# The chunk scan of an S5 layer: steps over chunk pairs against one hardware scan per 16 groups in a turned frame

## The chip, the cores and the metric

One core of one Trainium2 chip runs the whole program in one launch. Its engines are PE (matmuls, "PEld" its weight loads), DVE (vector), ACT (scalar functions and copies), POOL (GpSimd, elementwise work at leisure) and SP, which here only issues transfers. POOL issues transfers too, so a transfer in its queue stands behind the arithmetic issued before it. The metric is the device time of one execution in microseconds (us). A run of the kernel before takes 1603.12 us (median of 3; 1601.82 to 1603.6).

## The reference

One inference step of two decoder layers of width 1024 over 512 prompt tokens and 8 sample sequences of 8 tokens. Layer 0 mixes tokens with HGRN2 (a gated recurrence with 8 heads of 128), layer 1 with S5 (a complex diagonal recurrence). Every layer goes on with a SwiGLU mixer and a gated per-layer embedding, with LayerNorms after the residuals. The part that the change is about:

```
lam = lax.complex(a_re, a_im)                       # 64 groups x 64 states
lam_bar = jnp.exp(lam * delta)                      # the decay of one token
b_bar = ((lam_bar - 1.0) / lam)[..., None] * lax.complex(b_re, b_im)
bu = einsum('btgc,gpc->btgp', u, b_bar)             # 16 channels of a group
bu = bu.at[:, 0].add(lam_bar * h0)
h_t = lam_bar * h_(t-1) + bu_t                      # associative scan over the tokens
y = einsum('btgp,gcp->btgc', h, c_mat).real + d_skip * u
y = gelu(y);  val, gate = split(y @ w_glu);  out = val * sigmoid(gate)
```

Outputs are the features of all tokens, the last HGRN2 states, and the last S5 states of the prompt and of each sample sequence.

## The kernel before

**Tiling.** The 576 tokens go in two blocks of 288 columns, features on the partitions, eight k tiles of 128. Block 0 holds the first 224 prompt tokens and the 64 sample tokens, block 1 the other 288 prompt tokens. Each product with a weight matrix is made of three matmuls (L297 to L299), from a rounded part (`whi`, `xh`) and the rest (`wlo`, `xl`) of both sides. Matmuls write to `mm` banks, of which there are four, and the order of instructions on an engine is that in which the program issues them; an engine waits in order.

**Weight stream.** Slots of 128x1024 are loaded into two `wraw` buffers (`w_dma`, L224, on SP; within the S5 stage on POOL), copied to `whi` by ACT (L198) and taken from the raw values into `wlo` by DVE (L201), by POOL in the S5 stage. A slot's load is issued when its buffer is free, in SP's queue behind what was issued before.

**Preparation of S5.** `s5_prep_steps` is a generator that the channel mixer of layer 0, `ffn(0)`, calls one or two steps at a time between its output tiles. It loads the parameters, makes the decay `lam_bar` = `er` * (`r1` + i `r0`) with an exponential and two sines on ACT (L195), its powers up to 8 (`lr`, `li`) and the coefficients on DVE, and a table that PE transposes (L1222), ACT copies to `wts` and POOL's queue stores to `wt_scratch` (L1225). Then it walks over 16 packs of four groups: `load` issues three loads on SP, `bc` (L1240), `wr` (L1242), which reads `wt_scratch` and so waits for its store, and `bT` (L1246); `inputs` (DVE, from `zw<-wr,bT`) makes the input weights, which POOL's queue stores to `zw_scratch` (L1280); `coeffs` and `lag_kernels` make the output weights (`cl_scratch`) and the products within a chunk (`mg_scratch`). In between the mixer goes on: DVE adds PE's output tiles to the residual (`xf<-xf,mm`, L204), which frees the banks.

**S5 stage.** A chunk is 8 tokens. `U` holds the inputs with rows (step, channel) and columns [group, chunk]; `HS[0]`, `HS[1]` (tiles `xl`) hold the states at the starts of the chunks, real parts on rows 0 to 63, imaginary parts on rows 64 to 127, 64 groups by 36 chunks. Block 0 has chunks 0 to 27 (`KA` = 28) and the 8 sample sequences, one chunk each. In order:
- `z_part(0)`: PE makes what each chunk adds to the state, ACT copies it to `HS` and `ZL`.
- The scan of block 0 on DVE: `many` adds to every other state the one before, advanced by `lam8` (the decay of one chunk); `pair_step` goes in thirteen steps two chunks at a time with `lam16`; `many` then fills in the states between. `advance` is a complex product and a sum in five operations. The temporaries lie in `spare`, in the place of XH of block 1 (named `xh`).
- `ple_proj`: projections of layer 1's embeddings on PE, sixteen tiles, each copied by ACT to `pj`; then POOL issues the load of the samples' initial states `h0` (tile `sm`, L1531), and DVE scales them into `HS[0]` (L1532).
- `z_part(1)`; the samples' last states on POOL (`last_samples`).
- `lag_part` (products within the chunks, both blocks, into `U`) and `out_part(0)` (products of states with the output weights, L1371, added to `U` on DVE, GELU on ACT, stored to scratch and loaded back by `y_load`). Between them `step(scan, ...)` issues pieces of block 1's scan, `last_states`, as many as the tables `SL` and `SO0` say.
- The gated projection: units of block 0 on PE; before the fourth of them what is left of the scan is issued (`settle("scan")`), and then `out_part(1)` for the eight octets.

Of the kernel before, what the change touches and what calls it, by code (L numbers as in the profile page):

```python
# [17 lines left out]
T = 576  # L18
# [49 lines left out]
SL = (0, 1, 1, 1, 1, 1, 1, 0)  # L68
SO0 = (1, 1, 1, 1, 2, 1, 1, 1)
SY0 = (1, 1, 1, 1, 1, 1, 1, 1)  # L70
# [12 lines left out]
def weight_order():  # L83
    """The 128 x 128 weight tiles (name, layer, k tile, first column) as they are consumed."""
# [56 lines left out]
def hybrid_decoder_kernel(ctx: ExitStack, tc: tile.TileContext, a: dict):  # L141
# [16 lines left out]
    # ---------------------------------------------------------------- constants  # L158
# [23 lines left out]
    # features of all tokens; tile k of block b is [:, b, k, :], but for HGRN2, which takes k tiles of all tokens  # L182
# [3 lines left out]
    # the float32r part of a block's features and the rest of them  # L186
# [22 lines left out]
    # ---------------------------------------------------------------- weight stream  # L209
    # Slots are split as buffers come free, paced by the matmuls issued: not before their load has had  # L210
    # time to arrive, not two at once, so that the engines that split them go on with other work.
# [15 lines left out]
    def w_conv(force=False):  # L227
        """Splits the next slot into a float32r part and the rest, if a buffer is free."""
# [73 lines left out]
    def unit(out, p, ks, rh, rl, blk, first=True, last=True):  # L302
        """One output tile of one token block: sum over the k tiles ks with weights from position p."""
# [6 lines left out]
    def units(outs, p, ks, rh, rl, blk):  # L310
        """Output tiles whose weights follow each other, all of them with one k tile before the next."""
# [11 lines left out]
    def tick():  # L323
        """Called every few matmuls: issues a little of what was put off until its inputs are there."""
# [47 lines left out]
    # ---------------------------------------------------------------- norms  # L372
    class LayerNorm:
        """LayerNorm over features of the block's tiles in xf: sums are taken about the mean of the
        first half of the features, which lies within one standard deviation of the mean."""
# [12 lines left out]
        def added(self, m):  # L388
            """Called when tile m of the block is final."""
# [18 lines left out]
        def tail(self):  # L408
# [5 lines left out]
            # squares about the mean of the first half, as the tiles come  # L414
# [55 lines left out]
    # ---------------------------------------------------------------- HGRN2  # L470
    def hgrn():
# [24 lines left out]
        # lower bounds: softmax over the layer axis (one layer), cumulative sum less its first row  # L496
# [26 lines left out]
        def proj(h):  # L523
# [25 lines left out]
        def pairs(x, l):  # L549
            """The first and the second half of each chunk of 2 l prompt tokens."""  # L550
# [8 lines left out]
        def decay(h, d, ps):  # L559
            """Logarithm of the decay, keys, and the decay's sums from the starts of chunks of four sizes."""  # L560
# [86 lines left out]
        def scan(h):  # L647
# [3 lines left out]
            # decayed keys, token-major  # L651
# [13 lines left out]
            # states of the prompt blocks  # L665
# [10 lines left out]
            # states of the sample sequences  # L676
# [14 lines left out]
            # scores, transposed: [s, t]  # L691
# [16 lines left out]
            # what the initial states add to the outputs of the sample sequences: of four sequences, the queries of  # L708
            # all with the state of each
# [13 lines left out]
            # outputs  # L723
# [18 lines left out]
            # RMS norm over the head and output gate  # L742
# [26 lines left out]
        # output projection; the last head's scan runs beside the k tiles of the others  # L769
# [72 lines left out]
    # ---------------------------------------------------------------- channel mixer  # L842
# [104 lines left out]
    # ---------------------------------------------------------------- per-layer embedding  # L947
    def embeddings(i, pool):
        """The layer's input embeddings; the second result splits them once they are loaded."""
# [23 lines left out]
    def ple_gate(i, pj, pp, segs, emit, wait, second=None):  # L973
        """Gates of the projected embeddings for the columns (block, from, to) of each segment, in their order;
        the result starts the norm of a segment. The norms of all segments but the last start by themselves,
# [479 lines left out]
    def layer0_to_1():  # L1455
# [51 lines left out]
        for half in range(2):  # L1507
            many(0, 2, KA // 2 - 1, half)
# [306 lines left out]
```

## Time and profile before

| | |
|---|---|
| Runs | 1603.12 us (1601.82 to 1603.6) |
| Span of the profiled execution | 1598.7 us |
| Median less this span | 4.4 us |
| PE busy | 1516.5 us, 95% of the span |
| DVE / ACT / POOL busy | 941.6 / 688.3 / 238.7 us |
| Preparation of S5, from the first sine's input to the store of `wt_scratch` | about 459 to 500 us |
| S5 stage, scans on DVE | block 0 909 to 948, block 1 948 to 1012 us |

The page splits the span into engines' busy times, groups of instructions (line, engine, operation, output <- inputs) and transfers. A view of waits tells for each engine whom it waited for; a timeline row gives start, duration, engine, line, work, and in brackets the idle time before it and who ended it. A row with "x3" covers three instructions in a row. The name of a tile is that of the first tile in its place or the one written: the states appear as `xl`, the scan's temporaries as `xh`.

### The profile page before, as it was taken

Reading aid. Unit: us, or ns where it says so; the run is one execution under the profiler, and the core shown is the slowest. Engines: PE = TensorE matmul, PEld = TensorE weight load, DVE = VectorE, ACT = ScalarE, POOL = GpSimd, SP = SyncE. Lnnn points to the kernel's source line nnn. Section 1 sums busy time; section 2 is a strip of 40 time slices with the busy share of each in tenths; the row PEclk is TensorE's granted clock in tenths of the full one; section 3 lists DMA queues with packets and bytes.
Section 4 is the critical chain, followed back from the end, with each engine's and each line's share of the span. In section 5 each row is a group of like instructions: output and inputs, shape, how many; then the busy total and the mean of one; then the engine's idle time right before and its main releaser. Section 6 shows DMA issues by size and latency. Waiting matters only on the chain.

```text
span 1598.7 us, 30007 instructions
## 1 busy us (share of the span) xinstructions
PE 1516.5 (95%) x12550; PEld 1469.0 (92%) x12550; DVE 941.6 (59%) x1833; ACT 688.3 (43%) x1159; POOL 238.7 (15%) x284
## 2 busy tenths in 40 slices
PE   7899999899999999999999965899999999999998
PEld 7898989778999999999989965799999999999997
DVE  5748475768547666753476799567533333334685
ACT  5646464646532233123278533336522232133375
POOL 1303020202000112360022432202000000000111
PEclk9999999999999999999999996899999999999999
DMA  5213122232225766752215973332222222223021
GB/s 184 102 61 108 69 100 75 83 114 82 77 73 138 211 190 181 199 156 93 93 67 190 162 281 93 88 106 80 67 80 93 80 80 80 93 80 119 28 79 59
DMA packets 96390, 175.59 MB, mean 110 GB/s; under 512 B 41792, under 2 KB 56816, under 8 KB 96256
## 3 DMA queue, kind: packets, MB, share of 16 engines
q1 hardware_dynamic: 87856, 149.56, 30.2%
q0 software_dynamic: 8400, 24.13, 5.3%
q8 instruction: 98, 1.61, 0.4%
q14 instruction: 36, 0.29, 0.1%
HBM read 148.72 MB, written 24.94 MB: 109 GB/s over the span
## 4 chain that ended last, share of the span: by engine, by line
PE 71%; DVE 18%; ACT 5%; issue 2%; DMA 1%; POOL 1%; SPq 0%; DVEq 0%; ACTq 0%; POOLq 0%
PE mm L297 23%; PE mm L298 22%; PE mm L299 22%; DVE b L576 2%; DVE xh L201 2%; DVE wlo L201 1%; DVE am L201 1%; DVE ac L201 1%; DVE xl L201 1%; DVE K L201 1%; DVE xf L201 1%; ACT whi L198 1%; DVE ln_q L201 1%; DVE ln_z L201 1%; PE tr L668 1%
## 5 line engine op out<-in xcount | busy, mean ns | idle before, releaser
L297 PE MATMUL mm<-xh,whi 128*128 128x288 f32 x2048 | 609.0, 297 | 7.9 <-ACT xh L198 4.4
L298 PE MATMUL mm<-xl,whi 128*128 128x288 f32 x2048 | 607.8, 297 | 4.8 <-POOL xl L201 3.4
L299 PE MATMUL mm<-xh,wlo 128*128 128x288 f32 x2048 | 606.0, 296 | 1.3 <-DVE wlo L201 1.3
L297 PEld LDWEIGHTS mm<-xh,whi 128*128 128x128 f32 x2048 | 387.3, 189 | 14.5 <-ACT xh L198 5.6
L298 PEld LDWEIGHTS mm<-xl,whi 128*128 128x128 f32 x2048 | 387.4, 189 | 7.4 <-POOL xl L201 4.5
L299 PEld LDWEIGHTS mm<-xh,wlo 128*128 128x128 f32 x2048 | 387.3, 189 | 1.5 <-DVE wlo L201 1.5
L198 ACT ACTIVATE whi<-wraw 128x1024 fp32r<-128x1024 f32 x208 | 218.7, 1053 | 226.4 <-PE mm L298 124.2
L201 DVE TENSOR_TENSOR wlo<-wraw,whi 128x1024 fp32r<-128x1024 f32 x200 | 246.1, 1247 | 29.9 <-ACT whi L198 27.1
L297 PE MATMUL mm<-hhi,whi 128*128 128x288 f32 x704 | 209.3, 297 | 0.0
L299 PE MATMUL mm<-hhi,wlo 128*128 128x288 f32 x704 | 207.5, 295 | 0.0
L298 PE MATMUL mm<-hlo,whi 128*128 128x288 f32 x704 | 207.3, 294 | 0.0
L201 DVE TENSOR_TENSOR fs<-fs,mm 128x288 f32<-128x288 f32 x88 | 40.0, 454 | 267.6 <-PE mm L299 258.4
L297 PEld LDWEIGHTS mm<-hhi,whi 128*128 128x128 f32 x704 | 132.1, 188 | 1.7 <-issue 1.4
L298 PEld LDWEIGHTS mm<-hlo,whi 128*128 128x128 f32 x704 | 132.1, 188 | 0.3
L299 PEld LDWEIGHTS mm<-hhi,wlo 128*128 128x128 f32 x704 | 132.0, 188 | 0.0
L297 PE MATMUL mm<-xhi,whi 128*128 128x288 f32 x384 | 122.6, 319 | 0.0
L298 PE MATMUL mm<-xlo,whi 128*128 128x288 f32 x384 | 114.6, 298 | 0.0
L299 PE MATMUL mm<-xhi,wlo 128*128 128x288 f32 x384 | 114.3, 298 | 0.0
L201 POOL TENSOR_TENSOR ln_s<-ln_s,xf 128x288 f32<-128x288 f32 x24 | 24.3, 1011 | 574.4 <-DVE xf L201 454.7
L198 ACT ACTIVATE hhi<-fs 128x288 fp32r<-128x288 f32 x88 | 38.9, 442 | 148.3 <-DVE fs L201 148.3
L195 ACT ACTIVATE fs<-mm,eps 128x288 f32<-128x288 f32 x88 | 44.1, 502 | 135.7 <-PE mm L299 135.6
L297 PEld LDWEIGHTS mm<-xhi,whi 128*128 128x128 f32 x384 | 73.2, 191 | 6.9 <-issue 4.4
(292 smaller groups left out, 2166.3 us busy)
## 6 DMA issues: line engine op xcount, KB each, us to landing
wraw<-in_w_dram SPq DMA_DIRECT2D x198, 512.0 KB
wraw<-in_w_dram POOLq DMA_DIRECT2D x10, 512.0 KB, 5.6
S<-in_s_dram SPq DMA_DIRECT2D x8, 512.0 KB
out_hgs_dram<-So SPq DMA_DIRECT2D x8, 512.0 KB
wr<-wt_scratch SPq DMA_DIRECT2D x16, 256.0 KB
bT<-in_s5bt_dram SPq DMA_DIRECT2D x16, 256.0 KB
cl_scratch<-cl POOLq DMA_DIRECT2D x16, 256.0 KB, 3.4
zw_scratch<-zw POOLq DMA_DIRECT2D x16, 256.0 KB, 6.3
```

The lines of the kernel that those rows point to most:

```text
L195: nc.scalar.activation(out, in_, func, bias=ZERO if bias is None else bias, scale=scale)
L198: nc.scalar.activation(out, in_, ACT.Copy)
L201: (eng or nc.vector).tensor_tensor(out, x, y, op=op)
L297: nc.tensor.matmul(out, whi, rhi, start=start, stop=False)
L298: nc.tensor.matmul(out, whi, rlo, start=False, stop=False)
L299: nc.tensor.matmul(out, wlo, rhi, start=False, stop=stop)
L576: nc.vector.tensor_tensor_scan(b[l], segm[l], L, 0.0, op0=OP.mult, op1=OP.add)
L668: nc.tensor.matmul(ps[:, j * 128:j * 128 + 128], kT[:, j, :], Vh[:, j, :], start=True, stop=True)
```

## The change

The decay of a chunk is written as a length times a direction, `lam8` = `rho` * (c + i z). In a frame that turns with the direction, the recurrence over chunks has the real factor `rho`, the same for real and imaginary parts, and DVE's instruction for a first-order recurrence along a row (`tensor_tensor_scan`) can do it.

1. **Table (in the preparation, all on POOL).** `rho` from `er`; the direction's powers 1, 2, 4 .. 32 chunks by squaring, each brought back to length 1 by one correction (`direction`): 81 operations of 128x64. Then `turns(half)` for each 32 groups: powers 0 to 35, by doubling (36 products and sums of 128x32xn, n = 1, 2, 4, 8, 16, 4), the sign of the imaginary part, and two stores to `tb_scratch`. `turns(0)` is called behind the powers `lr`, `li`, `turns(1)` behind the coefficients, ahead of the table for `wt_scratch`. The tiles of the second half are those of the first. `lam16` with its four DVE operations goes.
2. **Load.** The table (C and Z, 1.18 MB each) comes by SP at the beginning of the S5 stage; Z takes the place of `spare`.
3. **Scan.** For each quarter of 16 groups: `turn` back (four DVE operations), one `tensor_tensor_scan` over 128x576, `turn` forward (four). The factors `rho`, 0 at each group's first chunk, lie in one buffer in the place of an earlier embedding; ACT fills it for the next quarter behind each scan (`lengths`). `SL` and `SO0` hand out block 1's scan in half quarters, seven of them, and what is left is issued before the gated projection begins.
4. **Around it.** `z_part(0)` has one copy less for each octet, and the state at block 1's start is copied once from `HS[0]`; the samples' initial states are scaled by ACT, not by DVE; both blocks' outputs come back into the place of `U[0]`.

```diff
-SL = (0, 1, 1, 1, 1, 1, 1, 0)
-SO0 = (1, 1, 1, 1, 2, 1, 1, 1)
-SY0 = (1, 1, 1, 1, 1, 1, 1, 1)
+SL = (0, 0, 1, 0, 1, 0, 1, 0)
+SO0 = (0, 1, 0, 1, 0, 1, 0, 1)
...
-    lam16 = const.tile([128, 2, NG], FP32, name="lam16")
+    rho = const.tile([128, NG], FP32, name="rho")
+    tb_d = nc.dram_tensor("tb_scratch", (128, 2, NG, 36), FP32).ap()
...
+        P = nc.gpsimd
+        pc, pz = (sp.tile([128, 6, NG], FP32, name=x) for x in ("pc", "pz"))
+        ta, tb = s64("ta"), s64("tb")
+
+        def square(c, z, c0, z0):
+            tt(ta, z0, z0, OP.mult, P)
+            tt(tb, c0, z0, OP.mult, P)
+            tt(c, c0, c0, OP.mult, P)
+            tt(c, c, ta, OP.subtract, P)
+            tt(z, tb, tb, OP.add, P)
+
+        def direction(c, z, first):
+            tt(ta, c, c, OP.mult, P)
+            tt(tb, z, z, OP.mult, P)
+            tt(ta, ta, tb, OP.add, P)
+            P.tensor_scalar(tb, ta, -0.5, 1.5, op0=OP.mult, op1=OP.add)
+            tt(c, c, tb, OP.mult, P)
+            tt(z, z, tb, OP.mult, P)
+            if first:
+                P.tensor_scalar(ta, ta, 0.5, 0.5, op0=OP.mult, op1=OP.add)
+                tt(rho, rho, ta, OP.mult, P)
+
+        tt(rho, er, er, OP.mult, P)
+        for _ in range(2):
+            tt(rho, rho, rho, OP.mult, P)
+        square(pc[:, 0], pz[:, 0], r1, r0)
+        for m in range(8):
+            if m > 1:
+                direction(pc[:, m - 2], pz[:, m - 2], m == 2)
+            if m < 2:
+                square(pc[:, 0], pz[:, 0], pc[:, 0], pz[:, 0])
+            elif m < 7:
+                square(pc[:, m - 1], pz[:, m - 1], pc[:, m - 2], pz[:, m - 2])
+
+        def turns(half):
+            gs = slice(32 * half, 32 * half + 32)
+            C, Z = (sp.tile([128, 32, 36], FP32, tag=x, name=x) for x in ("tC", "tZ"))
+            P.memset(C[:, :, 0:1], 1.0)
+            P.memset(Z[:, :, 0:1], 0.0)
+            for m in range(6):
+                n0 = 1 << m
+                n = min(n0, 36 - n0)
+                sh = [128, 32, n]
+                bc, bz = (x[:, m, gs, None].to_broadcast(sh) for x in (pc, pz))
+                A, B = (sp.tile([128, 32, 16], FP32, tag=x, name=x)[:, :, 0:n] for x in ("tA", "tB"))
+                c0, z0, c, z = C[:, :, 0:n], Z[:, :, 0:n], C[:, :, n0:n0 + n], Z[:, :, n0:n0 + n]
+                tt(A, c0, bc, OP.mult, P)
+                tt(B, z0, bz, OP.mult, P)
+                tt(c, A, B, OP.subtract, P)
+                tt(A, z0, bc, OP.mult, P)
+                tt(B, c0, bz, OP.mult, P)
+                tt(z, A, B, OP.add, P)
+            P.tensor_scalar(Z, Z, NSG, None, op0=OP.mult)
+            nc.gpsimd.dma_start(tb_d[:, 0, gs], C)
+            nc.gpsimd.dma_start(tb_d[:, 1, gs], Z)
...
+        turns(0)
...
-        tt(lam16[:, 0], lr[:, 8], lr[:, 8], OP.mult)
...
+        turns(1)
...
+    def turn(blk, q, back):
+        gs, n = slice(16 * q, 16 * q + 16), slice(1, 36 if blk else KA + 1)
+        h, c, C, Z = (x[:, n] if len(x.shape) == 2 else x[:, :, n] for x in
+                      (HS[blk][:, gs], s5["c"], s5["C"][:, gs], s5["Z"][:, gs]))
+        tt(c[0:64], h[64:128], Z[64:128], OP.mult)
+        tt(c[64:128], h[0:64], Z[0:64], OP.mult)
+        tt(h, h, C, OP.mult)
+        tt(h, h, c, OP.add if back else OP.subtract)
+
+    def lengths(q):
+        copy(s5["rho"][:, :, 1:36], rho[:, 16 * q:16 * q + 16, None].to_broadcast([128, 16, 35]))
+
+    def run_on(blk, q):
+        h = HS[blk][:, 16 * q:16 * q + 16].rearrange("p g k -> p (g k)")
+        nc.vector.tensor_tensor_scan(h, s5["rho"].rearrange("p g k -> p (g k)"), h, 0.0, op0=OP.mult, op1=OP.add)
+        lengths((q + 1) % 4)
...
-        for half in range(2):
-            many(0, 2, KA // 2 - 1, half)
-        for j in range(1, KA - 1, 2):
-            pair_step(j)
-        for half in range(2):
-            many(0, 1, KA // 2 - 1, half)
+        for q in range(4):
+            turn(0, q, True)
+            run_on(0, q)
+            turn(0, q, False)
+        copy(HS[1][:, :, 0], HS[0][:, :, KA])
...
-        nc.vector.tensor_scalar(HS[0][:, :, KA:36], h0, NSG, None, op0=OP.mult)
+        act(HS[0][:, :, KA:36], h0, ACT.Identity, scale=NSG)
...
-            for half in range(2):
-                many(1, 0, 18, half)
+            for q in range(4):
+                turn(1, q, True)
+                run_on(1, q)
                 yield
-            for j in range(KA - 1, 63, 2):
-                pair_step(j)
...
+                turn(1, q, False)
                 yield
...
-        tails["scan"] = scan
+        run(scan)
```

How the instructions move. First POOL's queue in the preparation; a row gives line, operation, output and input, shape (`par`, `sd`: parameters; `tA`, `tB`, `tC`, `tZ`: the table's tiles). Before:

```order
L1135 DMA par<-in_s5p_dram 128x192
L1137 DMA sd<-in_s5d_dram 128x16
L1225 DMA wt_scratch<-wts 128x4x128
L1302 DMA mg_scratch<-zt 1024x1x16
L1266 DMA cl_scratch<-cl 128x4x128
L1280 DMA zw_scratch<-zw 128x512
```

With the change, the last rows of the table and what follows:

```order
L200 TENSOR_TENSOR tB<-tC,pz 128x32x4
L200 TENSOR_TENSOR tZ<-tA,tB 128x32x4
L1224 TENSOR_SCALAR tZ<-tZ,sgn 128x1152
L1225 DMA tb_scratch<-tC 128x1152
L1226 DMA tb_scratch<-tZ 128x1152
L1281 DMA wt_scratch<-wts 128x4x128
L1358 DMA mg_scratch<-zt 1024x1x16
L1322 DMA cl_scratch<-cl 128x4x128
L1336 DMA zw_scratch<-zw 128x512
```

All of the table stands between the parameters' loads and the store of `wt_scratch`, and the stores of the other tables follow as before.

Then ACT's queue around the projections (`pj`), from the last copies of `z_part(0)` (`xl`, `zl`) to the first of `z_part(1)`. Before:

```order
L198 ACTIVATE xl_9912<-mm 128x8x27
L198 ACTIVATE xl_9913<-mm 128x8
L198 ACTIVATE zl<-mm 128x8x8
L198 ACTIVATE pj_10233<-mm 128x288 x7
L198 ACTIVATE whi<-wraw 128x1024
L198 ACTIVATE pj_10233<-mm 128x288 x7
L198 ACTIVATE whi<-wraw 128x1024
L198 ACTIVATE pj_10233<-mm 128x288 x2
L198 ACTIVATE xl_9913<-mm 128x8x35
```

With the change (`pr` is the buffer of factors, `sm` the samples' states):

```order
L197 ACTIVATE xl_10107<-mm 128x8x35
L197 ACTIVATE zl<-mm 128x8x8
L197 ACTIVATE pr_10106<-rho 128x16x35 x4
L197 ACTIVATE xl_10108<-xl_10107 128x64
L197 ACTIVATE pj_10352<-mm 128x288 x7
L197 ACTIVATE whi<-wraw 128x1024
L197 ACTIVATE pj_10352<-mm 128x288 x7
L197 ACTIVATE whi<-wraw 128x1024
L197 ACTIVATE pj_10352<-mm 128x288 x2
L194 ACTIVATE xl_10107<-sm,eps,sgn 128x64x8
L197 ACTIVATE xl_10108<-mm 128x8x35
```

Four refills of the factors and the copy of block 1's first state stand ahead of the projections' copies, and the scaling of the samples' states behind them. Lines up to 1070 are one less than before, since a table is gone.

More of the change, by code (lines that the diff above doesn't have):

```diff
@@ L1199, in s5_prep_steps @@
         V.tensor_copy(lam8[:, 1], li[:, 8])
-        tt(lam16[:, 0], lr[:, 8], lr[:, 8], OP.mult)
-        tt(t1, li[:, 8], li[:, 8], OP.mult)
-        tt(lam16[:, 0], lam16[:, 0], t1, OP.subtract)
-        stt(lam16[:, 1], lr[:, 8], 2.0, li[:, 8], OP.mult, OP.mult)
+        turns(1)
         cA, cB, c1, c2 = q, u, r1, dl
@@ L1384, in z_part @@
         if blk == 0:
-            copy(HS[0][:, g, 1:KA], v[:, :, 0:KA - 1])
-            copy(HS[1][:, g, 0:1], v[:, :, KA - 1:KA])
+            copy(HS[0][:, g, 1:36], v[:, :, 0:35])
             copy(ZL[:, g, 0:8], v[:, :, KA:36])
@@ L1439, in advance @@
         tt(out, m, c, OP.add, eng)
-    def many(blk, x0, n, half):
-        gs = slice(32 * half, 32 * half + 32)
-        w = [t[:, 0:32 * n].rearrange("p (g n) -> p g n", n=n) for t in s5["work"]]
-        x, y = (HS[blk][:, gs, i:i + 2 * n - 1:2] for i in (x0, x0 + 1))
-        advance(y, x, y, n, w, gs=gs)
-    def pair_step(j):
-        advance(chunk_state(j + 2), chunk_state(j), chunk_state(j + 2), lam=lam16)
+    def turn(blk, q, back):
[12 more added lines that the diff above has]
+        lengths((q + 1) % 4)
     s5 = {}
@@ L1487, in layer0_to_1 @@
         mg, cl = [octet(op, mg_d, o, "mg", OCT) for o in range(OCT)], []
-        spare = {}
-        chunk_tiles("xh", spare, 1)
-        spare = spare[1].rearrange("p g k -> p (g k)")
-        s5["work"] = [spare[:, T * i:T * i + T] for i in range(2)]
+        s5["C"] = op.tile([128, NG, 36], FP32, name="turn")
+        turn_z = {}
+        chunk_tiles("xh", turn_z, 1)
+        s5["Z"] = turn_z[1]
+        for n, x in enumerate((s5["C"], s5["Z"])):
+            nc.sync.dma_start(x.rearrange("p g k -> p (g k)"), tb_d[:, n].rearrange("p g k -> p (g k)"))
+        s5["rho"], s5["c"] = (x for x in s5["zp"].tile([128, 2, 16, 36], FP32, tag="praw", name="pr2").rearrange(
+            "p n g k -> n p g k"))
         settle(0)
@@ L1497, in layer0_to_1 @@
         nc.vector.memset(HS[0][:, :, 0:1], 0.0)
+        nc.vector.memset(s5["rho"][:, :, 0:1], 0.0)
+        lengths(0)
         for o in range(8):
@@ L1552, in last_states @@
         def last_states():
-            for half in range(2):
-                many(1, 0, 18, half)
+            for q in range(4):
+                turn(1, q, True)
+                run_on(1, q)
                 yield
-            for j in range(KA - 1, 63, 2):
-                pair_step(j)
-                if j == KA - 1:
-                    advance(chunk_state(KA), chunk_state(j), chunk_state(KA))
+                turn(1, q, False)
                 yield
@@ L1563, in last_states @@
             nc.gpsimd.dma_start(a["s5o"], po)
-            for half in range(2):
-                many(1, 1, 17, half)
-                yield
+            yield
         scan = last_states()
@@ L1576, in y_start @@
                 step(y_loads[b, o - 2])
-        yt = [[spare[:, (4 + o % 4) * NB:(5 + o % 4) * NB] for o in range(8)],
-              [U[0][:, 8 * o:8 * o + 8].rearrange("p g k -> p (g k)") for o in range(8)]]
+        yt = [[U[0][:, 8 * o:8 * o + 8].rearrange("p g k -> p (g k)") for o in range(8)]] * 2
         for o in range(8):
@@ L1609, in layer0_to_1 @@
                 if (blk, m) == (0, 3):
-                    settle("scan")
                     st.update(queue=nc.sync, lo=nc.vector, load=LOAD_MM, split=SPLIT_MM)
```

## The prediction

> **What bounds the kernel now.** I read the page's totals first, then PE's waits (for whom it waited, us in total, times, longest) in the two stretches that the change touches: the channel mixer of layer 0, where the S5 coefficients are made in the background (420 to 860 us), and the S5 stage (940 to 1015).
>
> ```profile
> span 1598.7 us, 30007 instructions
> PE 1516.5 (95%) x12550; PEld 1469.0 (92%) x12550; DVE 941.6 (59%) x1833; ACT 688.3 (43%) x1159; POOL 238.7 (15%) x284
> ...
> PE tr L432 <- DVE ln_q L201: 1.4, 1, 1.4
> PE mm L297 <- DVE xf L201: 1.3, 1, 1.3
> PE tr L1222 <- DVE wri L201: 0.7, 1, 0.7
> ...
> PE mm L1371 <- DVE u L201: 16.0, 2, 15.6
> PE mm L1371 <- DVE gs L201: 7.0, 1, 7.0
> ```
>
> PE is busy for 95% of the span, so whatever stops PE lengthens the run. In the first stretch no wait is longer than 1.4 us: the preparation is wholly hidden. In the S5 stage PE waits 23.0 us in three places, all on DVE, and that is all a shorter scan can win there. The price of the change therefore hangs on whether the new GpSimd table stays hidden in the first stretch.
>
> **The preparation.** Between the sine that feeds the table and the store of `wt_scratch`, POOL had nothing to do. These are timeline rows (start, us, engine, line, work, idle before it and who ended it):
>
> ```profile
> 461.88 0.35 ACT L195 ACTIVATE r<-r,eps 128x64 f32<-128x64 f32 x1 [3.20 <-DVE r L1158]
> 492.45 0.38 SPq L1240 DMA_DIRECT2D bc<-in_s5bc_dram  x1
> 500.14 0.78 POOL L1225 DMA_DIRECT2D wt_scratch<-wts  x1 [51.52 <-ACT wts L198]
> 502.94 0.72 SPq L1242 DMA_DIRECT2D wr<-wt_scratch  x1
> 504.45 0.38 SPq L224 DMA_DIRECT2D wraw<-in_w_dram  x1
> 511.27 0.69 DVE L201 TENSOR_TENSOR zw<-wr,bT 128x512 f32<-128x512 f32 x1 [2.98 <-DMA bT<-in_s5bt_dram]
> 513.22 0.45 DVE L204 SCALAR_TENSOR_TENSOR xf<-xf,mm 128x288 f32<-128x288 f32 x1
> 516.51 0.46 DVE L204 SCALAR_TENSOR_TENSOR xf<-xf,mm 128x288 f32<-128x288 f32 x1 [0.91 <-PE mm L299]
> 528.20 0.45 DVE L204 SCALAR_TENSOR_TENSOR xf<-xf,mm 128x288 f32<-128x288 f32 x1 [1.10 <-PE mm L299]
> ...
> wt_scratch<-wts POOLq DMA_DIRECT2D x1, 256.0 KB, 2.8
> zw_scratch<-zw POOLq DMA_DIRECT2D x16, 256.0 KB, 6.3
> ```
>
> The store goes out at 500.14, lands 2.8 us later, and SP, which issued `bc` at 492.45, is let go at 502.94. Behind `wr` on SP stand the load of `bT` and the next weights (504.45). DVE's `zw` starts 11.1 us after the store, and in DVE's queue behind it stands the fourth residual, done at 513.67, 13.5 us after the store. Now the whole table stands ahead of that store on POOL, so all of this moves with it.
>
> How late may it be? The rows at 516.51 and 528.20 are four output tiles apart, both let go by PE: 2.92 us a tile. The first is the sixth tile; with four `mm` banks PE can do the seventh, until 519.4, and then needs the bank that the fourth residual empties. 519.4 − 513.67 = 5.8 us of slack: a store later than **505.9** stops PE by the difference. The weights are no earlier bound: their load moves with the store as the residual does.
>
> How long does the table take? Prices of POOL (rows by tile, lowest/median/highest ns, and by line, total and mean) and DVE's load at that time:
>
> ```profile
> L201 POOL TENSOR_TENSOR KL<-KL,k x24: 717/734/1707, 46.9 to 309.9; 128x256 f32<-128x256 f32 x24
> L201 POOL TENSOR_TENSOR wlo<-wraw,whi x8: 2352/2398/2852, 898.9 to 1005.7; 128x1024 fp32r<-128x1024 f32 x8
> L493 POOL MEMSET ats<- x2: 152/152/152, 4.2 to 4.7; 128x64 f32 x2
> L201 POOL TENSOR_TENSOR xl<-xf,xh 128x288 fp32r<-128x288 f32 x32 | 32.7, 1021 | 149.7 <-ACT xh L198 134.7 <-PE mm L298 15.0
> L201 POOL TENSOR_TENSOR KH<-KH,k 128x576 f32<-128x576 f32 x8 | 16.1, 2018 | 256.2 <-ACT KH L195 256.2
> 952.98 1.59 POOL L201 TENSOR_TENSOR sm<-sm,zl 128x512 f32<-128x512 f32 x1
> 954.65 1.66 POOL L201 TENSOR_TENSOR sm<-sm 128x512 f32<-128x512 f32 x1
> 462.00:500.00 38.00, 37.27 (x283) 37.05 (x283) 27.83 (x116) 12.13 (x21) 0.00 (x0) 1.00 0.26 88
> ```
>
> The line through 128x256 (0.734) and 128x1024 (2.398) is 0.18 us plus 2.17 ns for each element of a row. Two operations of which one needs the other stand 0.08 us apart (954.65 − 952.98 − 1.59). At 288 columns the line gives 0.80 and the row 1.021, a factor of 1.27, when DVE works beside it; at 576 it gives 1.43 against 2.018, a factor of 1.41. DVE is busy 27.83 of the 38 us (window row: PE, its loads, DVE, ACT, POOL), so I take 1.27 while DVE runs on, and 1 once it stands still behind the wait.
> - Powers and directions: of 81 operations of 128x64, 78 wait for the sine. 78 × (0.18 + 0.14 + 0.08 = 0.40, less the overlap of the third that need no predecessor, so 0.36) = 28, times about 1.2: **34**.
> - Each half of the table: 36 products of 6720 elements in all, 36 × 0.18 + 14.6 = 21.1; gaps 1.9; the sign over 128x1152, bounded by the line at 2.7 and by a memset's rate at about 1.5: 2; two memsets 0.3; two stores to issue, 0.78 each, 1.6. **27**, twice 54.
> - The second half's tiles are the first half's, so its memsets wait until 590 KB twice have been stored. The nearest row is 256 KB in 6.3: **6**, with 3 to 10 as bounds.
>
> 94 us after 462.2 is 556.2, against 505.9: PE stands still for **50 us**. Low bound: the small operations at the memset's 0.152 (12), halves without gaps or contention (2 × 24), a wait of 3: 64, a loss of 20. High bound: 28 × 1.41 + 2 × 27 × 1.41 + 10 = 125, a loss of 81.
>
> The Trainium skill ("SBUF — State Buffer", section "Who interferes with whom") says that a DVE instruction with two SBUF inputs and a GpSimd instruction that reads SBUF shut each other out for a whole instruction; the pair of rows at 910.52 and 911.02 below agrees. Without any such shutting out the sum below would be about 1647.
>
> The Trainium skill ("GPSIMD Engine Reference", section 2.1 on instruction dispatch) gives about 6 us for the first call of a freshly loaded GpSimd kernel; no run here shows it, and with it the sum would be about 1659.
>
> After a long stand PE's clock has to come back. Windows after the 15.6 us wait (PE, its loads, DVE, ACT, POOL, then the granted clock):
>
> ```profile
> 985.00:990.00 5.00, 5.00 (x23) 5.00 (x22) 4.68 (x12) 1.70 (x5) 2.75 (x4) 0.50 0.68 123
> 990.00:995.00 5.00, 5.00 (x39) 5.00 (x39) 4.79 (x8) 3.35 (x4) 4.21 (x4) 0.99 0.01 2
> ```
>
> Half clock for 5 us loses 2.5 (23 matmuls against 39); I take **+3**, bounds 0 and 5.
>
> **The scan.** Rows of DVE, ACT, POOL and PE in the S5 stage, one from the chain of waits (911.02), one by tile (L576) and one of the transfers:
>
> ```profile
> 910.52 2.72 POOL L201 TENSOR_TENSOR wlo<-wraw,whi 128x1024 fp32r<-128x1024 f32 x1
> 911.02 2.68 DVE xh L201
> ...
> 909.33 4.35 DVE L201 TENSOR_TENSOR xh<-xl,lam 128x416 f32<-128x416 f32 x3
> 944.12 0.59 DVE L201 TENSOR_TENSOR xl<-xh 128x416 f32<-128x416 f32 x1
> 947.73 0.48 DVE L1532 TENSOR_SCALAR xl<-sm,sgn 128x512 f32<-128x512 f32 x1
> 961.32 0.76 DVE L201 TENSOR_TENSOR xl<-xh 128x576 f32<-128x576 f32 x1
> 1010.89 0.73 DVE L201 TENSOR_TENSOR xl<-xh 128x544 f32<-128x544 f32 x1
> 983.75 0.44 DVE L201 TENSOR_TENSOR u<-u,mm 128x288 f32<-128x288 f32 x1
> 1012.03 3.26 PE L1371 MATMUL mm<-xl,zw 128*64 128x64 f32 x56 [6.95 <-DVE gs L201]
> 910.59 1.32 ACT L198 ACTIVATE pj<-mm 128x288 f32<-128x288 f32 x4 [5.10 <-POOL xf L201]
> ...
> L576 DVE TENSOR_TENSOR_SCAN b<-seg,L x32: 1325/1342/1359, 36.6 to 301.5; 128x576 f32<-128x576 bf16 x32
> sm<-in_h_dram POOLq DMA_DIRECT2D x1, 256.0 KB, 5.2
> ```
>
> Block 0 took DVE from 909.33 to about 947.7 (38.4 us). Now: 32 products of 128x448 at 0.627 (between 0.59 at 416 and 0.76 at 576) and four scans of 1.34, 25.4, and once 2.1 for a split beside it (2.68 − 0.60): ends at 937. But the four copies of `rho` that ACT makes, one behind each scan, now stand ahead of the sixteen copies of `pj`, which empty PE's banks for the projections. These start at 937 and not at 910.6, so the projections end 26 us later, near 949; the load of `h0` waits for them and takes 5.2: 954.4, and with ACT's scaling and the first copies of `z_part(1)` block 1 begins at about 956, where it was 948.1.
>
> Block 1 was on DVE until 1011.6. Now: 32 × 0.74 + 4 × 1.34 = 29.1; until the last output of block 0 three quarters of it (21.8), seven additions of 0.44 (3.1), and three splits now on POOL beside them at 2.1 (6.3): its `u` comes at 987.2, not 983.75. PE's gated work took 21.3 us from there (1012.03 − 6.95 = 1005.1), so that block 1's outputs can start at 1008.5, when DVE has long done (956 + 29.1 + 6.3 + 5.3 = 996.7). They started at 1012.03: **−3**. Bounds: −12, if `u` is not held back, and +5, if each of ACT's turns costs more.
>
> The table's loads (2 × 1.18 MB on SP) stand behind `mg` and ahead of the input stores; at 2.8 to 6.3 us for 256 KB over single queues they take some 10 to 25 us, beside the products and norms of 860 to 909, which last 49: nothing, and up to 10 if the stores of the inputs are late by it. The four operations less for `lam16` are 4 × 0.3 off the path: nothing.
>
> **Sum.** 1598.7 + 50 + 3 − 3 = 1648.7; the median of the runs, 1603.12, lies 4.4 above the profiled span: **1653**.
>
> **Rivals.**
> - *The table is hidden.* It decides at one point, a store before 505.9, so a table of at most 43.7 us. For it: POOL is idle for 51.52 us there, and a memset of the same size takes 0.152. Against it: the 13440 elements of the halves at 2.17 ns (29) and the wait for the stores (6) leave 9 for 150 instructions. Then only the scan is left, with −3 to −12: 1600, down to 1591. Chance 0.12.
> - *The table stalls, but the scan gives back all of PE's 23.0 us of waits.* For it: both waits name DVE, and DVE's work falls by some 47 us. Against it: the projections on ACT. 1653 + 3 − 23 = 1633. Chance 0.14.
> - *ACT's queue makes the scan stage worse*: each `rho` copy holds the next scan and all that stands behind it, block 1's `u` comes at 1001 and not at 987, and its outputs 21.3 later at 1022, 10 behind before. 1653 + 3 + 10 = 1666. Chance 0.10.
> - *The table is longer than its high bound*, since products of 32 strips with 1 or 2 elements cost more than a row of 64: 130 us and more, 1690 and up. Chance 0.08.
>
> The forecast itself has 0.56. Low: a table of 64 with −8 in the scan, 1598.7 + 20 + 3 − 8 + 4.4 = 1618; high: a table of 125, 1598.7 + 81 + 3 + 1 + 4.4 = 1688. That holds the second and third rival and leaves out the first and the last, 0.20 together. A measurement of this kernel tells 0.2% (3.2 us) from no change. Of the first rival's 0.12 I put 0.09 on faster and 0.03 on within that bound; all else is slower: 0.88.
>
> **What would show it.** Right: POOL busy without a break from 462 to about 550, `wt_scratch` stored there, `wr` on SP right behind it, and a PE wait of about 50 us for DVE `xf` near 519, with a granted clock of about 0.5 for some us after. In the S5 stage, `pj` starts near 937 plus the shift, and PE's wait for `gs` before block 1's outputs is gone. Wrong: a `wt_scratch` store within 44 us of the sine, or no PE wait there; POOL's small operations well under 0.3 or over 0.6 us; `pj` copies that start where they did.

## The result, and the profile after

The changed kernel takes 1653.87 us (median of 4; 1651.65 to 1657.98) against 1603.36 (1601.82 to 1605.06): a ratio of 1.0312, with a 95% interval of 1.0293 to 1.033. It is slower by 50.5 us, where 50 had been forecast (1653.0).

The page of the changed kernel: span, busy time of the engines, and, of the 40 slices, PE's share and its granted clock.

```profile
span 1656.2 us, 30048 instructions
PE 1522.3 (92%) x12550; PEld 1474.6 (89%) x12550; DVE 929.8 (56%) x1701; ACT 693.2 (42%) x1162; POOL 319.1 (19%) x447
PE   8899999999996299999999928899999999999998
PEclk9999999999998599999999968899999999999999
```

POOL has 80 us more work and DVE 12 less. In PE's slices a hole has come at 497 to 580 us, slices 13 and 14, with the clock down beside it. The old hole in the S5 stage, now mostly in slice 24, has kept about its size.

PE's waits in the two stretches, the mixer of layer 0 first and then the S5 stage (for whom, us in total, times, longest):

```profile
PE mm L296 <- DVE xf L203: 43.6, 1, 43.6
PE tr L1278 <- DVE wri L200: 3.7, 3, 1.9
...
PE mm L296 <- ACT pj L197: 32.0, 1, 32.0
```

In the first stretch one wait of 43.6 us for the residual stands where there was none over 1.4. In the second, the old waits for `u` and `gs` (23.0) are gone, and one of 32.0 us for ACT's `pj` has come; the next longest there is 4.1.

Where the time went is read from first and last starts of groups by tile. Of the kernel before (name, number, shortest/median/longest ns, first and last start): `fs` of the mixer, products of `z_part(0)` (xh) and of `out_part` (xl), the norms' `ln_z`.

```profile
L195 ACT ACTIVATE fs<-mm,eps x88: 482/502/505, 403.8 to 1475.3; 128x288 f32<-128x288 f32 x88
L1371 PE MATMUL mm<-xh,zw x256: 198/222/270, 896.2 to 904.6; 128*64 128x64 f32 x112, 128*64 128x36 f32 x16
L1371 PE MATMUL mm<-xl,zw x512: 198/225/370, 948.3 to 1021.9; 128*64 128x64 f32 x150, 128*64 128x36 f32 x21
L201 DVE TENSOR_TENSOR ln_z<-xf,ln_q x64: 443/451/1068, 369.9 to 1557.4; 128x288 f32<-128x288 f32 x64
```

Of the changed kernel:

```profile
L194 ACT ACTIVATE fs<-mm,eps x88: 477/502/505, 407.5 to 1532.8; 128x288 f32<-128x288 f32 x88
L1427 PE MATMUL mm<-xh,zw x256: 198/222/270, 951.7 to 960.0; 128*64 128x64 f32 x112, 128*64 128x36 f32 x16
L1427 PE MATMUL mm<-xl,zw x512: 198/222/271, 1028.8 to 1076.1; 128*64 128x64 f32 x150, 128*64 128x36 f32 x21
L200 DVE TENSOR_TENSOR ln_z<-xf,ln_q x64: 444/451/1071, 373.7 to 1614.9; 128x288 f32<-128x288 f32 x64
```

The profiled execution of the changed kernel is 3.7 us late before the change has done anything (407.5 − 403.8; it is the longest of the four). From there:

| Stretch (us) | before | changed | difference |
|---|---|---|---|
| preparation: first `fs` to first product of `z_part(0)` | 492.4 | 544.2 | +51.8 |
| S5 stage: to the last product of `out_part(1)` | 125.7 | 124.4 | −1.3 |
| rest: to the last `ln_z` | 535.5 | 538.8 | +3.3 |

The preparation carries the whole loss. Its timeline in the changed kernel (start, us, engine, line, work, idle before it and who ended it):

```profile
465.58 0.35 ACT L194 ACTIVATE r<-r,eps 128x64 f32<-128x64 f32 x1 [3.20 <-DVE r L1158]
466.01 0.37 POOL L200 TENSOR_TENSOR tb<-r,r 128x64 f32<-128x64 f32 x1 [3.26 <-ACT r L194]
497.14 0.16 POOL L1209 MEMSET tC<- 128x32 f32 x1
525.99 0.54 POOL L1226 DMA_DIRECT2D tb_scratch<-tZ  x1
528.65 0.15 POOL L1209 MEMSET tC<- 128x32 f32 x1 [2.12 <-DMA tb_scratch<-tC]
530.06 0.15 POOL L1210 MEMSET tZ<- 128x32 f32 x1 [1.26 <-DMA tb_scratch<-tZ]
555.18 0.78 POOL L1281 DMA_DIRECT2D wt_scratch<-wts  x1
...
560.25 0.73 SPq L1298 DMA_DIRECT2D wr<-wt_scratch  x1
568.92 0.69 DVE L200 TENSOR_TENSOR zw<-wr,bT 128x512 f32<-128x512 f32 x1 [48.64 <-DMA bT<-in_s5bt_dram]
570.87 0.44 DVE L203 SCALAR_TENSOR_TENSOR xf<-xf,mm 128x288 f32<-128x288 f32 x1
```

From the sine's end (465.93) to the store, POOL has no gap longer than about 0.1 us but for the 3.4 us in which the second half waits for the first half's stores. Powers take until 497, the first half until 526.5, the second from 530 to 555.2. SP, DVE and then PE stand in a row behind the one store, as the prediction had them.

### The profile page after: what moved, and what is told of

It reads as the page before. It is cut to its first block, busy times and chain, and to the rows that moved or that the text cites. A ratio compares the mean times of both kernels' runs of the same rounds, so it can differ in the third digit from the quotient of the medians.

```text
span 1656.2 us, 30048 instructions
## 1 busy us (share of the span) xinstructions
PE 1522.3 (92%) x12550; PEld 1474.6 (89%) x12550; DVE 929.8 (56%) x1701; ACT 693.2 (42%) x1162; POOL 319.1 (19%) x447
## 3 DMA queue, kind: packets, MB, share of 16 engines
q1 hardware_dynamic: 88144, 151.92, 29.8%
## 4 chain that ended last, share of the span: by engine, by line
PE 68%; DVE 12%; POOL 6%; ACT 5%; issue 5%; DMA 3%; SPq 0%; DVEq 0%; POOLq 0%; ACTq 0%
PE mm L296 21%; PE mm L297 21%; PE mm L298 21%; DVE b L575 2%; DVE wlo L200 1%; DVE K L200 1%; DVE xf L200 1%; ACT whi L197 1%; PE mm L1427 1%; POOL tA L200 1%; POOL tB L200 1%; DVE ln_q L200 1%; DVE ln_z L200 1%; PE tr L667 1%; DMA u<-y_scratch 1%
## 5 line engine op out<-in xcount | busy, mean ns | idle before, releaser
L296 PE MATMUL mm<-hhi,whi 128*128 128x288 f32 x704 | 211.6, 301 | 43.6 <-DVE xf L203 43.6
L296 PEld LDWEIGHTS mm<-hhi,whi 128*128 128x128 f32 x704 | 134.2, 191 | 45.6 <-DVE xf L203 43.9
L200 POOL TENSOR_TENSOR ln_s<-ln_s,xf 128x288 f32<-128x288 f32 x24 | 24.3, 1011 | 572.6 <-DVE xf L200 451.3
```

The source lines that it names most:

```text
L200: (eng or nc.vector).tensor_tensor(out, x, y, op=op)
L296: nc.tensor.matmul(out, whi, rhi, start=start, stop=False)
```

## Experiments

Each kernel is timed against the one before on the same chip, whose medians there lie between 1603.2 and 1603.8. The stretches named below are those of the table above.

| Run | Edit | us | ratio to before (95%) |
|---|---|---|---|
| changed kernel | | 1653.87 | 1.0293 to 1.033 |
| e1 | table in pieces behind the packs | 1602.91 | 0.999 to 1.0011 |
| e3 | block 0's refills on POOL | 1645.69 | 1.0249 to 1.0286 |
| e5 | old scan, table alone | 1655.0 | 1.0305 to 1.0336 |
| e7 | `wt_scratch` stored by SP | 1641.89 | 1.0212 to 1.0256 |
| e6 | old scan, half the table | 1625.42 | 1.0116 to 1.0157 |
| e8 | e1, and DVE for what waited on ACT | 1592.08 | 0.9926 to 0.9959 |
| e9 | e8, scan handed out earlier | 1602.01 | 0.998 to 1.0004 |
| e10 | e8, all refills on DVE | 1592.22 | 0.9917 to 0.9944 |
| e11 | e10, outputs before the scan | 1596.48 | 0.994 to 0.9965 |
| e12 | e10, samples on DVE | 1592.66 | 0.9918 to 0.9945 |
| e13 | e12, outputs between | 1593.68 | 0.9925 to 0.995 |

The theory was that the loss is the table's place on POOL's queue, ahead of the store that SP waits for. The rivals were that the work costs wherever it stands, since it slows DVE, and that the scan stage, with its new wait of 32.0 us, is what costs.

**The same table elsewhere (e1).** The work of `turns` becomes a generator, and one piece is issued behind each pack's `zw_scratch` store; only powers and directions stay ahead of `wt_scratch`.

```diff
-        turns(0)
-        turns(1)
...
                 inputs(i - 1)
+                next(table, None)
                 yield
```

> The changed kernel, with the powers and directions where they are, but the two halves of the table cut into twelve pieces, one on POOL's queue behind the zw_scratch store of each pack, so that only the 81 small operations stand ahead of the wt_scratch store. If the loss is the table's place ahead of that store (the theory), the one wait of 43.6 us for xf and its clock go: 1653.9 less about 51, 1602, and what is left against before is the scan stage alone, -1 to +3. If the table costs by its work beside DVE wherever it stands, some 75 us of POOL work at a factor of 1.2 to 1.4 come out of DVE: 1615 to 1625. If the scan stage with its wait of 32.0 us for pj is what costs, less than half goes: 1635 or more.

Measured: 1602.91, 51.0 less than the changed kernel and equal to before. The preparation takes 493.1, against 492.4 before and 544.2 changed. The store's row in this run, and the longest of PE's waits in the stretch:

```profile
502.17 0.83 POOL L1285 DMA_DIRECT2D wt_scratch<-wts  x1 [7.28 <-ACT wts L197]
...
PE tr L431 <- DVE ln_q L200: 1.4, 1, 1.4
```

POOL is done with the powers 7.28 us before `wts` is there. The table's operations run beside DVE all the same, and cost nothing that shows beyond 0.7 us of the preparation: the loss is their place in the queue.

**The table alone (e5), and half of it (e6).** In the kernel before, with its own scan, the same code on POOL, whose result nothing reads: in e5 both halves, in e6 the powers and `turns(0)` only.

> The kernel before with its own scan, and only the table made on POOL as in the change and stored to tb_scratch, where nothing reads it. Theory: the whole loss without the scan's part, 50 to 54 above before: 1653 to 1658. Rival (the loss is shared with the scan stage): 1620 to 1635.

> The kernel before with its own scan; on POOL the powers, the directions and the first half of the table only, all ahead of the wt_scratch store. In the changed kernel the first half's second store had been issued 60.6 us after the sine (526.5 against 465.9); 462.2 + 60.6 = 522.8, so by the rule 'loss = store time less 505.9' it loses 17, and 3 for PE's clock: 1618 to 1626. Rival (the loss goes with the amount of POOL work, in proportion to the 51.6 of the whole table, 61 of 89 us): 1637 to 1640.

Measured: e5 1655.0, a preparation of 543.7, and the S5 stage as before (126.0). So the table alone costs 51.3, and the new scan neither adds to the loss nor takes from it. e6: 1625.42, within the 1618 to 1626 of the rule and 12 below the proportional rival; its preparation is 22.0 longer, where the rule gave 20.

The store's row and PE's wait in e6:

```profile
525.26 0.78 POOL L1285 DMA_DIRECT2D wt_scratch<-wts  x1
...
PE mm L297 <- DVE xf L204: 12.1, 1, 12.1
```

This execution is 2.2 us late ahead of the table (first `fs` at 406.0), so the store stands at 523.1 in the time of the kernel before, 17.2 past the limit of 505.9. With 61 of the 89 us of work ahead of the store, about two thirds, the loss is 22.0 of 51.8, about four tenths. From e6 to the changed kernel the store is 28.4 later (551.5 − 523.1) and the loss 29.8 larger; in e1, with the store at 500.9 in the same time, there is none to speak of. So it is a threshold and then about one for one.

**One store taken out of the queue (e7).** SP issues the store of `wt_scratch`; all else stays.

```diff
-        nc.gpsimd.dma_start(wt_d.rearrange("(j q) k -> q j k", j=4), wts)
+        nc.sync.dma_start(wt_d.rearrange("(j q) k -> q j k", j=4), wts)
```

> The changed kernel, with the one store of wt_scratch issued by SP and not by POOL; the table stays ahead of all other stores on POOL. Theory (the whole queue is late, not the one store): wr comes in time, but the store of the first zw_scratch still goes out behind the table, at about 557, and the second zw needs its buffer: DVE stands there about 35 us and PE with it: 1635 to 1645. Rival (the one store is the whole matter): 1602 to 1608.

Measured: 1641.89. Rows of POOL, SP and DVE:

```profile
558.23 0.56 POOL L1336 DMA_DIRECT2D zw_scratch<-zw  x1
...
507.88 0.73 SPq L1298 DMA_DIRECT2D wr<-wt_scratch  x1
...
564.92 0.69 DVE L200 TENSOR_TENSOR zw<-wr,bT 128x512 f32<-128x512 f32 x1 [34.53 <-DMA zw_scratch<-zw]
```

`wr` comes at 507.88 and not at 560.25, and DVE then stands for 34.5 us one pack later, since the store that empties its `zw` buffer is behind the table too. The preparation is still 37.2 longer than before. It is the whole queue that is late, not the one store.

**The refills in block 0 (e3).** In the changed kernel, POOL refills the factors of block 0's scan and DVE copies block 1's first state.

```diff
-        lengths((q + 1) % 4)
+        lengths((q + 1) % 4, None if blk else nc.gpsimd)
...
-        copy(HS[1][:, :, 0], HS[0][:, :, KA])
+        nc.vector.tensor_copy(HS[1][:, :, 0], HS[0][:, :, KA])
```

> The changed kernel, with the factors of block 0's scan refilled by POOL and not by ACT, and the state at block 1's start copied by DVE, so that nothing that waits for the scan stands ahead of the pj copies on ACT. The table is left where it is. Theory: the wait of 32.0 us for pj goes; block 1's scan starts when block 0's has ended, 17 us earlier than now, and PE's waits for u and gs come back with up to half of that: 1636 to 1645. Rival (the projections' late end was cover for a scan that binds anyway): 1650 to 1656.

Measured: 1645.69, 8.2 less and just outside the theory's 1636 to 1645. The wait of 32.0 us for `pj` is gone, but one of 20.6 has come in its place; PE's wait and the rows behind it:

```profile
PE mm L1427 <- ACT zl L197: 20.6, 1, 20.6
...
993.25 1.11 POOL L1511 COPY pr<-rho 128x560 f32<-128x560 f32 x1 [6.00 <-DVE xl L1517]
997.91 0.54 POOL L1602 DMA_DIRECT2D sm<-in_h_dram  x1
...
1001.88 0.81 ACT L194 ACTIVATE xl<-sm,eps,sgn 128x512 f32<-128x512 f32 x1 [22.95 <-DMA sm<-in_h_dram]
```

The same illness one engine on: the refills now hold POOL's queue, behind them the load of the samples' states is issued at 997.91, ACT waits for it 22.95 us, and the copies of `z_part(1)` stand behind that on ACT.

**Both mended (e8), and the scan earlier (e9).** e1, and in the S5 stage block 0's refills, the copy and the samples' scaling on DVE. e9 is e8 with SL = (1, 1, 1, 1, 0, 0, 0, 0) and SO0 = (1, 0, 1, 0, 1, 0, 1, 0).

```diff
-        lengths((q + 1) % 4)
+        lengths((q + 1) % 4, None if blk else nc.vector)
...
-        act(HS[0][:, :, KA:36], h0, ACT.Identity, scale=NSG)
+        nc.vector.tensor_scalar(HS[0][:, :, KA:36], h0, NSG, None, op0=OP.mult)
```

> The changed kernel with the table in twelve pieces behind the packs, and in the S5 stage with block 0's refills of the factors, the copy of block 1's first state and the scaling of the samples' states on DVE, so that no ACT instruction that waits for the scan stands ahead of pj or of z_part(1), and the load of the samples' states is not behind anything that waits for the scan on POOL. Theory: neither the wait of 31.2 us for pj nor the 20.6 us for zl that came in its place; block 1's scan starts some 13 to 15 us earlier: 1586 to 1592. Rival (DVE's scan binds the stage whichever order the others have): 1598 to 1603.

> The same as the run before it, with block 1's scan handed out earlier: SL = (1,1,1,1,0,0,0,0), SO0 = (1,0,1,0,1,0,1,0), so that two quarters are ahead of block 0's outputs and not one and a half. If the end of the scan is what block 1's outputs wait for, up to 3 us less; if block 0's outputs are, which now stand behind half a quarter more, 3 us more; within 2 us of it otherwise.

Measured: e8 1592.08, at the upper edge of the theory's range and 11.3 faster than the kernel before (0.9926 to 0.9959): both waits are gone, and the S5 stage takes 112.8, 12.9 less than before. e9, of which 3 either way was expected, is 9.9 slower than e8. The same wait is the largest in both, and in sum 5.5 us longer in e9; of e8, PE's wait and ACT's rows, and then PE's wait of e9:

```profile
PE mm L1461 <- ACT u L197: 14.7, 1, 14.7
...
956.49 0.67 ACT L197 ACTIVATE pr<-rho 128x560 f32<-128x560 f32 x1 [15.21 <-DVE xl L1524]
957.06 1.29 ACT L197 ACTIVATE u<-mm 128x288 f32<-128x288 f32 x4
```

```profile
PE mm L1461 <- ACT u L197: 20.2, 2, 13.4
```

Block 1's refills are still on ACT, and the copies that empty PE's banks of the lag products stand behind one of them in e8, behind two in e9. That is 5.5 of the 9.9; the rest lies in smaller waits, of which one of 4.6 for a load of `u` is new, and its cause stays open.

**What is left (e10 to e13).** e10 puts block 1's refills on DVE too. e11 adds SL = (1, 1, 0, 0, 0, 0, 0, 0) and no step of the scan between block 0's outputs. e12 is e10 with the samples' five operations on DVE (SE = 0); e13 is e12 with e11's SL and SO0 = (0, 0, 1, 0, 0, 1, 0, 1).

> The spread table and the S5 stage with DVE (1592.1), now with block 1's refills of the factors on DVE too (0.45 us each), so that ACT's copies of the lag products (u) do not stand behind a refill that waits for the scan. Theory: the wait of 14.7 us for ACT's u and the 3.6 behind it go; of these, three quarters of the scan still stand ahead of block 0's last outputs on DVE and take back more than half: 1583 to 1588. Rival (DVE's scan is what binds): 1591 to 1594.

> The same, with one quarter of block 1's scan ahead of block 0's outputs (SL = (1,1,0,0,0,0,0,0)) and the other three behind all of them (SO0 all 0), beside the first three units of the gated projection. Theory: the gated projection of block 0 starts some 10 us earlier, and the rest of the scan, 22 us and up to 6 of port losses, ends about when PE is done with these units: 1578 to 1585. Rival (block 1's outputs then wait for the scan): no better than the run before, 1584 to 1592.

> The spread table with all refills on DVE (1592.2), and the five operations for the samples' last states on DVE and not on POOL. Beside them the first quarter of block 1's scan took 12.4 us on DVE where the same six rows take 6.3 alone; on DVE they cost about 5 x 0.70 = 3.5 and up to 4.2 with the two halves of the product apart. If the two engines shut each other out (the theory), 2 to 4 us are won, 1588 to 1590; if the slower rows have another cause, the run gets slower by 3 to 4, 1595 to 1596.

> The same, with one quarter of block 1's scan ahead of block 0's outputs, one and a half between them and the rest behind (SL = (1,1,0,0,0,0,0,0), SO0 = (0,0,1,0,0,1,0,1)). In the run with all outputs first, PE had the gated projection early but then waited 17.3 us for gs, which stood on DVE behind three quarters of the scan; with one and a half quarters left behind them this wait should be about half, and the outputs about 6 us earlier than where they are: 1583 to 1588. Rival (what is won at the outputs is given back at gs in full): 1588 to 1592.

Measured: 1592.22, 1596.48, 1592.66 and 1593.68: none better than e8. e10 is its rival; e11 is slower than both of its ranges, e12 lies between its two, and e13 is 1.7 above the upper end of its rival. PE's longest waits in the stage, in the order e10, e11, e13 (e12 has one of 11.5 for DVE's `u`):

```profile
PE mm L1434 <- DVE u L200: 13.5, 2, 13.1
```

```profile
PE mm L296 <- ACT gs L194: 17.3, 1, 17.3
PE mm L1434 <- DVE u L200: 9.2, 1, 9.2
```

```profile
PE mm L296 <- ACT gs L194: 8.7, 1, 8.7
PE mm L1434 <- DVE u L200: 8.1, 2, 7.4
```

The wait moves from ACT's `u` to DVE's `u` to `gs` as the order changes, and the stage takes 112.8 us in e8, 113.3 in e10, 118.8 in e11, 112.3 in e12 and 115.7 in e13. DVE ends the scan with `po` at 994.70 in e8, 996.15 in e10, 998.36 in e11, 993.98 in e12 and 993.20 in e13; counted from the first product of the stage that is after 95.6, 96.9, 100.7, 95.9 and 96.3 us. Of these rows, e8's and e13's:

```profile
994.70 0.26 DVE L1638 TENSOR_SCALAR po<-po,sgn 128x64 f32<-128x64 f32 x1
```

```profile
993.20 0.26 DVE L1638 TENSOR_SCALAR po<-po,sgn 128x64 f32<-128x64 f32 x1
```

This fits a stage that is bound by DVE's chain of two scans, where the order of the others only says where PE waits for it: the slowest, e11, ends the scan latest. But it is argued, not shown, since no run shortens the chain clearly, and e13 ends the scan as early as e10 and the stage 2.4 later. e12 did shorten the first quarter: its scan took 1.36 where e10's took 2.24 beside POOL, and `po` is 1.0 earlier counted from the stage's start; the time is the same within the scatter, so what holds the stage in e12 and e13 is left open.

## Why the prediction was right, point by point

**The place and the mechanism.** The chain store, `wr`, `zw`, fourth residual, bank was as written, and e1, e5, e6 and e7 each take one link of it: the table without its place costs nothing that shows, the place without the new scan costs all, half the table costs its lateness and not its work, and the store freed alone meets the next one in the queue.

**The size.** 94 us of table were forecast, 89.2 measured (555.18 − 465.93), with parts that missed on both sides:

| Part | forecast | measured |
|---|---|---|
| powers and directions | 34 | 31.2 |
| first half, beside DVE | 27 | 29.4 |
| wait for the stores | 6 | 3.5 |
| second half, DVE still | 27 | 25.1 |

The sum of the parts hides two misses. Most of the small operations were 0.29 to 0.32 us where the line gave 0.32, but they followed one another faster than priced: the eleven from 475.53 to 479.00, beside which DVE made no split, took 0.32 each with their gaps, not 0.36. At that pace the 77 from 466.01 to 497.14 are 24.3 us and not 28. They took 31.1, so what DVE did to them was a factor of 1.28, not 1.2. The base was priced too high and the factor too low. The first half of the table was meant to have a factor of 1.27 too, but its 27 has none in it; it took 29.4 where the second half, the same work with DVE still, took 25.1. The wait for the stores came out near its lower bound, since the later of the two stores of 590 KB landed 4.1 us after its issue (530.06 − 525.99).

Behind the store it went the other way: the transfer took 5.07 until SP moved (560.25 − 555.18), not 2.8, with the table's own stores just ahead of it; in e6, where they are too, it took 5.1, and in e1, where they are not, 3.2. The fourth residual was done 16.1 us after the store, not 13.5. PE ran dry at 571.4 − 43.6 = 527.8, or 524.1 in the time of the kernel before, 4.7 later than forecast. That is no gain. The 24 operations for `wri`, which PE transposes into the table for `wts`, took DVE 6.8 us beside POOL, where they take 4.3 in the kernel before and in e1 with POOL idle. So PE had waited for them 3.7 us, not 0.7, and had then run at a lower clock for some us (0.66 from 505 to 510, below).

So the wait is the store's lateness past 505.9 (551.5 − 505.9 = 45.6, where 50 were forecast), plus the 2.6 behind it, less the 4.7: 43.6 measured. With 3.0 of longer waits for `wri` and 4.7 us by which PE was busy longer in the preparation (493.6 against 488.9 for as many matmuls), that is 51.3 of the 51.8; 50 and 3 for the clock had been forecast. That the time came within 1 us of the forecast is in part luck: a store that came 4.7 earlier than priced, a way behind it that was 2.6 longer and a scan term that came out 1.7 smaller (below) nearly cancel.

The Trainium skill ("GPSIMD Engine Reference", section 2.1 on instruction dispatch) would have added about 6 us for the first call of a freshly loaded kernel. The first operation of the table, at 458.26, took 0.29 us after 5.60 us of waiting for its input, so nothing of that shows here; POOL had made the same kind of operation much earlier in the program (`KL<-KL,k`, from 46.9 in the kernel before).

**The clock.** Windows behind PE's waits for `wri` and behind its long wait (PE, its loads, DVE, ACT, POOL, granted clock, DMA, GB/s):

```profile
505.00:510.00 5.00, 4.00 (x20) 4.00 (x21) 3.61 (x10) 2.82 (x4) 4.69 (x7) 0.66 0.01 3
571.00:576.00 5.00, 4.63 (x19) 4.64 (x20) 4.88 (x11) 1.56 (x3) 1.33 (x2) 0.50 0.84 245
576.00:581.00 5.00, 5.00 (x39) 4.64 (x38) 3.93 (x9) 0.47 (x1) 1.92 (x3) 0.87 0.93 316
```

19 matmuls in 5 us at half clock, 39 in the next: 2.6 us, where 3 had been taken. The size came out, but by luck: the row at 985 that it was read from is not the recovery from the wait of 15.6 us. In the kernel before that wait ended at 969.38, and 985 comes 16 us later, behind a row of shorter waits (975 to 984, 0.5 to 1.8 us each). Of that kernel:

```profile
969.38 4.64 PE L1371 MATMUL mm<-xl,zw 128*64 128x64 f32 x96 [15.59 <-DVE u L201]
970.00:975.00 5.00, 4.59 (x108) 4.48 (x106) 4.67 (x19) 1.67 (x4) 0.00 (x0) 0.70 0.27 85
```

A mean of 0.70 is 3 of the 5 us at half clock, so the clock was back at about 973, 3.6 us after PE had gone on. After the 43.6 us it was back at about 577.3 (0.87), 5.9 us after. What sets this length stays open.

**The scan.** −3 was forecast and −1.3 measured in the stage, with the steps on DVE and ACT in place but not PE's. In the time of the kernel before (less 55.5), block 0's scan took DVE 28.6 us (27.5 forecast); the projections' copies began when it had ended; block 1's scan began at 956.9 (956). The rows:

```profile
992.20 0.67 ACT L197 ACTIVATE pr<-rho 128x560 f32<-128x560 f32 x1 [6.02 <-DVE xl L1513]
995.09 1.29 ACT L197 ACTIVATE pj<-mm 128x288 f32<-128x288 f32 x4
...
1012.44 2.60 DVE L200 TENSOR_TENSOR pr<-xl,xh 64x560 f32<-64x560 f32 x2 [17.66 <-ACT xl L197]
...
1068.63 7.66 PE L1427 MATMUL mm<-xl,zw 128*64 128x64 f32 x256
```

Block 1's outputs were to start at 1008.5, 3.5 earlier than before. They started at 1068.63, or 1013.1 in the time of the kernel before, 1.1 later. The stage is shorter only because they then took 7.66 us where they had taken 10.08 behind a wait of 6.95, at a granted clock of 0.73 (1012 to 1022; here 1.00). So a measured −1.3 beside a forecast of −3 is luck.

The prediction had the lateness of `pj` and of `h0`, but did not say that PE would stand for it: 32.0 us, in place of the 23.0 for `u` and `gs`. That is also what is true of the rival "the scan gives back all of PE's 23.0 us of waits": the scan does give them back, and ACT's queue takes them again. e8 shows what the scan is worth without that: 12.9.

**What missed.** The rest of the program, 3.3 longer in the profiled execution, had no term. The traces show where they lie: from 10 to 20 us behind the last product of `out_part(1)`, PE did 48 matmuls at a granted clock of 0.83 where it had done 72 at 1.00, and 24 matmuls at the full pace of 0.13 us are 3.2 us. e3 and e7 have the same dip (0.66) and a rest of 539.6 and 541.6; in e1, e5 and e6 the clock is 1.00 there, with 62 to 68 matmuls, and the rest 536.0 to 536.8. Why the clock dips in some kernels and not in others stays open. Among the expectations, e3 lies just outside its range, e9 missed by its price, and e10 to e13 won nothing over e8: the waits were read one by one, and not the chain that they may all be cut from.

## What to carry to other kernels

Work put on an idle engine is free only as long as nothing that others wait for stands behind it in that engine's queue, its transfers too: look for the first thing queued behind it, work out its latest time (here 505.9), and put the work behind it in pieces. The same holds for small copies that wait for a chain: on ACT and on POOL they held the copies that empty PE's banks or a load, and on the engine that the chain runs on they cost 0.45 us each (up to 2.47 beside POOL's products, in e8). When a wait goes and another of like length comes, ask whether both are cut from one chain before reordering again.

## What the runs showed of the hardware

Unexpected was how POOL and DVE disturb each other here: mostly not by a common factor, but by whole instructions. The same operation of the table, beside a DVE product and without one:

```profile
481.26 1.27 POOL L200 TENSOR_TENSOR pz<-tb 128x64 f32<-128x64 f32 x1
485.77 0.29 POOL L200 TENSOR_TENSOR pz<-tb 128x64 f32<-128x64 f32 x1
...
479.81 2.57 DVE L200 TENSOR_TENSOR wlo<-wraw,whi 128x1024 fp32r<-128x1024 f32 x2
```

Most of the small operations ran at 0.29 to 0.32 us. Six took 1.15 to 1.30, in three pairs, which end at 470.35, 482.53 and 497.19; DVE made three pairs of `wlo` splits in that time, which end at 470.20, 482.38 and 497.01. The Trainium skill ("SBUF — State Buffer", section "Who interferes with whom") says that a DVE instruction with two SBUF inputs contends with a GpSimd instruction that reads SBUF, and calls the ports that they share an exclusive lock. The trace agrees: a short operation beside one long split takes about as long as the split. In sum the short operations took 1.28 times their undisturbed time, close to the 1.27 that the prediction had read from a longer one (128x288).

A `tensor_scalar` over 128x1152 took 3.2 us on POOL, though DVE stood still, where the line of the two-operand products gives 2.7: one operand less was no gain there. The short `tensor_scalar` with two constants took 0.24 over 128x64, less than the products; which of length and kind of operand makes the difference was not tested.

```profile
550.88 3.20 POOL L1224 TENSOR_SCALAR tZ<-tZ,sgn 128x1152 f32<-128x1152 f32 x1
```
